# Two chunks of each SwiGLU computed with the tokens held still and turned by the DMA crossbar

## The chip, the cores and the metric

The kernel runs on one core of a Trainium2 chip. Five engines matter: TensorE (PE, matmuls; its weight loads are PEld), VectorE (DVE), ScalarE (ACT), GpSimd (POOL) and SyncE (SP), which here only starts transfers. The metric is the device time of one execution in microseconds. Before the change the median of three runs is 724.2 us (722.27 to 726.59).

## The reference, cut to what matters

One layer for 256 tokens of width 1024 in fp32: a SwiGLU, a mixer (Mamba-2 and differential attention side by side), and a second SwiGLU, each between two RMSNorms.

```
def swiglu(x, w_gate, w_up, w_down):
    return (jax.nn.silu(x @ w_gate) * (x @ w_up)) @ w_down
h = h + 0.5 * rmsnorm(swiglu(rmsnorm(h, ffn1_pre_g), ffn1_w_gate, ffn1_w_up, ffn1_w_down), ffn1_post_g)
...
h = h + 0.5 * rmsnorm(swiglu(rmsnorm(h, ffn2_pre_g), ffn2_w_gate, ffn2_w_up, ffn2_w_down), ffn2_post_g)
```

w_gate and w_up are 1024x2816, w_down is 2816x1024. The change touches only these two SwiGLUs, called f1 (0 to 187 us of the profiled execution) and f2 (537 to 722 us).

## The kernel before, in words

**Precision.** Each fp32 operand is split into a high part (an ACT cast to fp32r) and a low part (a DVE subtraction of that from the operand). A product is three matmuls: high by high, low by high, high by low. Every weight that comes in from memory therefore costs one ACT cast and one DVE subtraction per 128x1024 piece before PE can use it.

**Gate and up.** The 2816 columns are taken in eleven chunks of 256, j = 0 to 10. Chunks 0 and 1 are computed together with the tokens stationary: the normed tokens u (high and low) are the weights that PE holds, and 512 columns of w_gate or w_up stream past (`mm_nat`, L482). Their result has tokens on the partitions, but the down projection needs the columns of FF on the partitions, so it is transposed: on PE in f1, and in f2 by the DMA crossbar, which takes 16-bit elements, so that an fp32 tile goes as two planes of 16 bits (`by_dma`: planes copy L1086, transpose L1087, copy back L1091). Chunks 2 to 10 are computed with the weights stationary (`mm_runs`, `mm_part` L441): per chunk and per gate or up, 16 matmuls of 512 columns (u high and u low side by side) and 16 of 256. The result is right for the down projection at once, but it lies in two halves of a PSUM bank, which are added by an ACT copy and a DVE addition (`taken_from`, L447 and L448), two of each for gate and two for up. Then come Silu on ACT, the multiplication of up by Silu(gate) on DVE (L1127), and the split of the result into high and low (`split`, L420 cast on ACT, L421 subtraction on DVE).

**Down.** The plan for both SwiGLUs is `q1 Q2 q3 Q0 ppp`: chunks 2g and 2g+1 form quad g, and four quads are multiplied by a Strassen-Winograd scheme of seven pieces of six matmuls each (168 matmuls, L939). Chunks 8, 9 and 10 are multiplied plainly after that (L777). The pieces need sums of weight quarters. For q1 and q3 DVE makes them as they are needed (`Quad`: sums wt L128, cast wqh L136, subtraction wql L142). For Q2 and Q0 they are made early, during the chunks ("kept" sums, `stored_sums`: POOL starts the loads of ws at L221, DVE subtracts at L226, L228, L231 and L233, POOL stores to a scratch in DRAM at L229 and L234), and are reloaded later and only split (`Stored`: cast L161, subtraction L162). Which of the four steps of the kept sums is taken in which chunk stands in two tables in `ffn`, one for the middle of a chunk and one for its end.

**What sets the order.** In these stages the order on each engine comes from the tile scheduler, which follows the order of the code and of its priorities; an engine runs its own list strictly in that order. Weights are split ahead: `take()` hands out the pieces for the next matmuls and has the splits of three chunks ahead put into the lists. Tiles come from pools: k4 has 29 slots of 4 KB (all split weights, weight sums, high and low results), k2 has 7 of 2 KB, raw (incoming weights) has 3, PSUM has 3 banks pj and 5 banks bg. A tile has to wait until its slot's last reader is done. When the last chunk's multiplication has been issued, two more weight pieces are put into the lists ahead of the split of its result.

In the rows below, names end in the SwiGLU and the chunk (gh_f210 is the high result of f2, chunk 10), or in the number of the weight load and the piece (wql1173 is the low part of piece 3 of the quad whose first load is number 117; in f2 loads 115 and 116 are q1, 117 to 120 are Q2, from 121 on q3).

## Time and profile before

| what | value |
|---|---|
| median of 3 runs | 724.2 us (722.27 to 726.59) |
| profiled execution | 724.1 us, span 722.4 us, granted clock 0.999 |
| PE busy | 713.9 us (99%) |
| DVE busy | 643.3 us (89%) |
| ACT busy | 493.8 us (68%) |
| POOL busy | 60.8 us (8%) |
| f1: gate and up of chunks 8, 9, then of 10 | 98.44 to 120.67, then to 131.78 us |
| f1: the four quads | 131.78 to 169.86 us |
| f2: gate and up of chunks 8, 9, then of 10 | 626.53 to 648.76, then to 659.87 us |
| f2: the four quads | 659.87 to 699.70 us |

Rows of a timeline read: start in us, duration in us, engine, line, operation, output tile and input tile, and in square brackets the idle time before it and what ended that. Instructions of one engine overlap a little, so that the step from one start to the next (1.13 us for the 1.22 us subtractions) is what an instruction costs in a queue. A row with xN stands for N instructions that follow each other.

### The profile page before, as it was taken

Reading aid. Unit: us, or ns where it says so; the run is one execution under the profiler, and the core shown is the slowest. Engines: PE = TensorE matmul, PEld = TensorE weight load, DVE = VectorE, ACT = ScalarE, POOL = GpSimd, SP = SyncE. Lnnn points to the kernel's source line nnn. Section 1 sums busy time; section 2 is a strip of 40 time slices with the busy share of each in tenths; the row PEclk is TensorE's granted clock in tenths of the full one; section 3 lists DMA queues with packets and bytes.
Section 4 is the critical chain, followed back from the end, with each engine's and each line's share of the span. In section 5 each row is a group of like instructions: output and inputs, shape, how many; then the busy total and the mean of one; then the engine's idle time right before and its main releaser. Section 6 shows DMA issues by size and latency. Waiting matters only on the chain.

```text
span 722.4 us, 10602 instructions
## 1 busy us (share of the span) xinstructions
PE 713.9 (99%) x3925; PEld 612.7 (85%) x3925; DVE 643.3 (89%) x994; ACT 493.8 (68%) x835; POOL 60.8 (8%) x110
## 2 busy tenths in 40 slices
PE   9999999999999999999999999999999999999996
PEld 7888888888888888899888788888888889888775
DVE  6989999999979999887996998679989599898996
ACT  5666666767856777879965577795667567466572
POOL 4501110000140000000000000000021010100000
PEclk9999999999999999999999999999999999999999
DMA  8969978878574467765564664564647679975861
GB/s 295 265 213 329 319 256 287 314 265 294 175 229 129 140 212 230 233 208 177 171 220 147 206 218 137 170 193 175 235 141 256 183 234 304 331 262 224 316 221 59
DMA packets 104436, 162.06 MB, mean 224 GB/s; under 512 B 7532, under 2 KB 73664, under 8 KB 103360
## 3 DMA queue, kind: packets, MB, share of 16 engines
q1 hardware_dynamic: 92880, 135.80, 56.8%
q0 software_dynamic: 6976, 24.00, 9.5%
q10 hardware_dynamic: 4528, 1.58, 1.0%
q8 instruction: 31, 0.51, 0.3%
q14 instruction: 21, 0.17, 0.1%
HBM read 150.85 MB, written 9.47 MB: 222 GB/s over the span
## 4 chain that ended last, share of the span: by engine, by line
PE 97%; DVE 2%; issue 0%; DVEq 0%; ACT 0%; ACTq 0%
PE pup_f L441 14%; PE pg_f L441 14%; PE pxs L441 6%; PE pws L482 6%; PE pgt L482 6%; PE acc_f1p L939 5%; PE acc_f2p L939 4%; PE pn_f L498 3%; PE pbc L441 3%; PE pk L441 3%; PE pq L441 3%; PE pn_mx L482 3%; PE pwd L482 3%; PE pn_f L482 3%; PE pz L441 2%; PE acc_f1p L777 2%
## 5 line engine op out<-in xcount | busy, mean ns | idle before, releaser
L360 DVE TENSOR_TENSOR wlo<-raw,whi 128x1024 fp32r<-128x1024 f32 x204 | 244.9, 1228 | 15.6 <-ACT whi L359 14.6
L359 ACT CAST whi<-raw 128x1024 fp32r<-128x1024 f32 x204 | 206.7, 1049 | 14.0 <-DMA raw<-in_ffn_w_gate_dram 5.2
L441 PE MATMUL pup_f<-u_f,whi 128*128 128x512 f32 x288 | 68.7, 391 | 0.0
L441 PE MATMUL pg_f<-u_f,whi 128*128 128x512 f32 x288 | 68.2, 389 | 0.0
L441 PEld LDWEIGHTS pg_f<-u_f,whi 128*128 128x128 f32 x288 | 54.1, 188 | 11.2
L441 PEld LDWEIGHTS pup_f<-u_f,whi 128*128 128x128 f32 x288 | 53.0, 188 | 10.2
L441 PEld LDWEIGHTS pg_f<-u_f,wlo 128*128 128x128 f32 x288 | 36.9, 191 | 1.4
L441 PE MATMUL pup_f<-u_f,wlo 128*128 128x256 f32 x288 | 37.6, 284 | 0.0
L441 PE MATMUL pg_f<-u_f,wlo 128*128 128x256 f32 x288 | 37.4, 283 | 0.0
L441 PEld LDWEIGHTS pup_f<-u_f,wlo 128*128 128x128 f32 x288 | 35.8, 192 | 0.1
L482 PE MATMUL pgt<-whi,u_mx 128*128 128x512 f32 x128 | 33.1, 393 | 0.0
L162 DVE TENSOR_TENSOR wql<-raw,wqh 128x1024 fp32r<-128x1024 f32 x28 | 32.8, 1222 | 0.3 <-ACT wqh L161 0.3
L420 ACT CAST gh_f<-sg_f 128x512 fp32r<-128x512 f32 x18 | 11.2, 621 | 30.8 <-DVE sg_f L1127 28.9
L441 PE MATMUL pxs<-u_mx,whi 128*128 128x512 f32 x128 | 29.9, 390 | 0.0
L447 ACT COPY su_f<-pup_f 128x256 f32<-128x256 f32 x36 | 13.4, 371 | 23.0 <-PE pup_f L441 22.8
L482 PEld LDWEIGHTS pgt<-whi,u_mx 128*128 128x128 f32 x128 | 23.6, 188 | 5.3 <-issue 0.7
L136 ACT CAST wqh<-wt 128x1024 fp32r<-128x1024 f32 x16 | 16.8, 1052 | 16.1 <-DVE wt L128 14.8
L441 PEld LDWEIGHTS pxs<-u_mx,whi 128*128 128x128 f32 x128 | 23.8, 188 | 4.8
L161 ACT CAST wqh<-raw 128x1024 fp32r<-128x1024 f32 x28 | 27.4, 1048 | 0.0
L515 ACT ACTIVATE s<-s,nm 128x128 f32<-128x128 f32 (+1 forms) x32 | 14.3, 447 | 11.2 <-DVE nm L1634 9.3
L1535 DVE TENSOR_TENSOR E<-E,cbm 128x768 f32<-128x768 f32 x16 | 15.3, 957 | 6.4 <-ACT E L515 6.4
L1440 DVE SCALAR_TENSOR_TENSOR xs<-xr,cols_b,xs 128x255 f32<-128x255 f32 (+2 forms) x48 | 20.5, 480 | 0.6 <-ACT xs L1437 0.3
(500 smaller groups left out, 1703.8 us busy)
## 6 DMA issues: line engine op xcount, KB each, us to landing
raw<-in_w_in_dram SPq DMA_DIRECT2D x40, 1024.0 KB, 5.1
raw<-in_ffn_w_gate_dram SPq DMA_DIRECT2D x20, 1024.0 KB, 6.1
raw<-in_ffn_w_up_dram SPq DMA_DIRECT2D x20, 1024.0 KB, 5.7
raw<-in_ffn_w_down_dram SPq DMA_DIRECT2D x18, 1024.0 KB, 6.5
ws<-in_ffn_w_down_dram POOLq DMA_DIRECT2D x16, 512.0 KB, 6.8
sums_f<-ws POOLq DMA_DIRECT2D x16, 512.0 KB, 6.2
raw<-sums_f SPq DMA_DIRECT2D x8, 1024.0 KB, 7.0
raw<-in_ssd_w_branch_dram SPq DMA_DIRECT2D x8, 1024.0 KB, 4.9
```

The costliest lines, as they stand in the source:

```text
L136: nc.scalar.copy(hi, src)
L161: nc.scalar.copy(hi, src)
L162: nc.vector.tensor_sub(lo, src, hi.bitcast(F32))
L359: last_cast[0] = behind(nc.scalar.copy(hi, r[:, js, :]), "cast").ins
L360: m = nc.vector.tensor_sub(lo, r[:, js, :], hi.bitcast(F32))
L441: nc.tensor.matmul(to, w_(j)[:, m * P:(m + 1) * P], x_(j), start=first and j == 0, stop=not first and j == KD - 1, skip_group_check=True)
L482: nc.tensor.matmul(acc, a(k0 + j), b(j), start=first and i == 0, stop=last and i == 11)
L498: nc.tensor.matmul(accs[b], x_(k0 + j), w_(j), start=first and j == 0 and w_ is wh and x_ is acts[b][0], stop=last and j == 3 and w_ is wl)
L777: nc.tensor.matmul(acc[b][q][:, cs] if to is None else to, x_[:, ts], w_(kt)[:, halves[q]][:, cs], start=to is not None and kt == 0 and x_ ...
L939: nc.tensor.matmul(bank[p], x_, w_, start=p not in begun, stop=last and p in (1, 5, 6, 7))
L1440: nc.vector.scalar_tensor_tensor(dst[:, m, s:], acc[:, m, :T - s], cw(3 - s, c), dst[:, m, s:], ALU.mult, ALU.add)
L1535: nc.vector.tensor_tensor(E, E, cbm[g].unsqueeze(1).to_broadcast([P, 2, 3 * P]), ALU.mult)
```

## The change

Chunks 8 and 9 of both SwiGLUs are taken together with the tokens stationary, as chunks 0 and 1 are. Their four weight loads (1024 rows by 256 columns, gate and up of one chunk in turn) become four of 512 rows by 512 columns, the two of gate first, then the two of up. Gate and up each take 48 matmuls of 512 columns in two banks, one for each block of 128 tokens. Silu reads the bank directly, DVE multiplies the up bank by it, ACT copies the result into two 16-bit planes (L1163) and starts a crossbar transpose (L1164). Later (`LATER = 3` half chunks after the block's own four, at most at the end of chunk 10) the landed planes are copied back together into a tile v (two copies, L1170), and v is split by one cast (L427) and one subtraction (L428) of 128x1024. In f2 the kept sums' steps are moved one to two chunks sooner; the tables of f1 stay, but are called from the new places.

```diff
+SOONER = ("f2",)
+NATURAL, LATER = {"f1": (8,), "f2": (8,)}, 3
...
         for j in range(2, FF // T):
-            t_chunk(wg[0], 0, j * T)
-            t_chunk(wu[0], 0, j * T)
+            if j in NATURAL[tag]:
+                for w in (wg, wu):
+                    for k0 in (0, 512):
+                        s_chunk(w[0], k0, j * T)
+            elif j - 1 not in NATURAL[tag]:
+                t_chunk(wg[0], 0, j * T)
+                t_chunk(wu[0], 0, j * T)
...
+        mids = {2: (0,), 3: (0,), 4: (0, 0), 5: (1,), 6: (1, 1), 7: (2,), 8: (2, 2), 9: (3,), 10: (3, 3)}
+        ends = {2: (0,), 3: (1,), 4: (0, 1), 5: (2,), 6: (1, 2), 7: (3,), 8: (2, 3), 10: (3,)}
+        if tag in SOONER:
+            store_sums((0, 0))
+            mids = {2: (0, 1), 3: (0, 1), 4: (1, 2), 5: (2,), 6: (2, 3), 7: (3,), 8: (3,)}
+            ends = {2: (0, 1), 3: (0, 1), 4: (1, 2), 5: (2,), 6: (2, 3), 7: (3,), 8: (3,)}
...
+        def by_tokens(j):
+            sg, n = [None] * 2, 0
+            for part, bank in (("g", pj), ("u", lambda name: bg([P, 512], name))):
+                accs = [bank(f"p{part}n_{tag}{j}{b}") for b in range(2)]
+                for i in range(2):
+                    w = take()
+                    for b in range(2):
+                        bs = slice(b * P, (b + 1) * P)
+                        mm_nat(accs[b], w, (lambda k: uh(k)[:, bs], lambda k: ul(k)[:, bs]), i * 4, i == 0, i == 1, "w")
+                        if i == 1 and part == "g":
+                            sg[b] = k2([P, 512], f"sgn_{tag}{j}{b}")
+                            act(sg[b], accs[b], AF.Silu)
+                        elif i == 1:
+                            nc.vector.tensor_tensor(sg[b], accs[b], sg[b], ALU.mult)
...
+            for b in range(2):
+                planes = k2([P, 2, 512], f"np_{tag}{j}{b}", U16)
+                lands.append(k2([P, 2, 4, P], f"nl_{tag}{j}{b}", U16))
+                nc.scalar.copy(planes, sg[b].bitcast(U16).rearrange("p (c h) -> p h c", h=2))
+                nc.scalar.dma_start_transpose(lands[b].rearrange("p h m t -> p (h m) t"),
+                                              planes.rearrange("p h c -> p (h c)"))
+            gu.extend([None] * 4)
+            yield
+            v = k4([P, 4, T], f"v_{tag}{j}")
+            for b in range(2):
+                nc.scalar.copy(v[:, :, b * P:(b + 1) * P].bitcast(U16).rearrange("p m (t h) -> p h m t", h=2), lands[b])
+            gh, gl = (k4([P, 4, T], f"g{x_}_{tag}{j}", F32R) for x_ in "hl")
+            split(gh, gl, v)
...
         for j in range(2, FF // T):
+            if j in NATURAL[tag]:
+                turning[min(done_chunks[0] + 4 + LATER, 2 * (FF // T - 2))] = t = by_tokens(j)
+                next(t)
+            if j in NATURAL[tag] or j - 1 in NATURAL[tag]:
+                continue
```

The list of ACT before, in f2 at the end of chunk 10 (wqh1154 is the last high part of q1, wqh1171 and on are those of Q2):

```order
L136 CAST wqh1154_6746<-wt1154_6742 128x1024
L161 CAST wqh1171_6750<-raw117_6623 128x1024
L161 CAST wqh1172_6793<-raw118_6689 128x1024
L161 CAST wqh1173_6797<-raw118_6689 128x1024
L420 CAST gh_f210_6666<-sg_f210_6668 128x512
L161 CAST wqh1175_6824<-raw119_6814 128x1024
L161 CAST wqh1177_6828<-raw119_6814 128x1024
```

The list of ACT now, at the same place:

```order
L163 CAST wqh1171_6655<-raw117_6538 128x1024
L163 CAST wqh1172_6698<-raw118_6597 128x1024
L163 CAST wqh1173_6702<-raw118_6597 128x1024
L427 CAST gh_f210_6574<-sg_f210_6576 128x512
L1170 COPY v_f28_6708<-nl_f280_6567 128x2x4x128
L1170 COPY v_f28_6708<-nl_f281_6571 128x2x4x128
L427 CAST gh_f28_6711<-v_f28_6708 128x1024
L163 CAST wqh1175_6734<-raw119_6724 128x1024
```

The two copies that bring the turned chunks back and the cast of their high part stand between the cast of chunk 10's result and the fourth high part of Q2; f1 has the same four rows at the same place.

The list of DVE before, same place in f2 (sg_f210 is the product of up and Silu(gate) of chunk 10):

```order
L1127 TENSOR_TENSOR sg_f210_6668<-su_f210_6733,sg_f210_6668 128x512
L162 TENSOR_TENSOR wql1173_6798<-raw118_6689,wqh1173_6797 128x1024
L421 TENSOR_TENSOR gl_f210_6667<-sg_f210_6668,gh_f210_6666 128x512
L233 TENSOR_TENSOR ws011_6561<-ws011_6561 128x512
L162 TENSOR_TENSOR wql1175_6825<-raw119_6814,wqh1175_6824 128x1024
L162 TENSOR_TENSOR wql1177_6829<-raw119_6814,wqh1177_6828 128x1024
```

The list of DVE now:

```order
L1205 TENSOR_TENSOR sg_f210_6576<-su_f210_6638,sg_f210_6576 128x512
L164 TENSOR_TENSOR wql1173_6703<-raw118_6597,wqh1173_6702 128x1024
L428 TENSOR_TENSOR gl_f210_6575<-sg_f210_6576,gh_f210_6574 128x512
L428 TENSOR_TENSOR gl_f28_6712<-v_f28_6708,gh_f28_6711 128x1024
L164 TENSOR_TENSOR wql1175_6735<-raw119_6724,wqh1175_6734 128x1024
L164 TENSOR_TENSOR wql1177_6739<-raw119_6724,wqh1177_6738 128x1024
```

The low part of the turned chunks now stands ahead of all further weight subtractions, and the last step of the kept sums (ws011, L233) has left this place; it now stands some forty rows earlier, in chunk 7.

The list of ACT now, in f2 after the matmuls of chunks 8 and 9 (sgn is their product, np the planes, nl where the transpose lands; wqh115x are the high parts of q1):

```order
L138 CAST wqh1151_6577<-raw115_6462 128x1024
L1163 COPY np_f280_6566<-sgn_f280_6476 128x1024
L138 CAST wqh1152_6581<-raw116_6504 128x1024
L1164 DMA_TRANSPOSE nl_f280_6567<-np_f280_6566 128x8x128
L1163 COPY np_f281_6570<-sgn_f281_6490 128x1024
L138 CAST wqh1153_6585<-raw116_6504 128x1024
L1164 DMA_TRANSPOSE nl_f281_6571<-np_f281_6570 128x8x128
L138 CAST wqh1155_6591<-wt1155_6587 128x1024
```

And before, at that place:

```order
L136 CAST wqh1151_6669<-raw115_6516 128x1024
L447 COPY su_f29_6614<-pup_f290_6625 128x256
L447 COPY su_f29_6614<-pup_f291_6626 128x256
L136 CAST wqh1152_6673<-raw116_6572 128x1024
L136 CAST wqh1153_6677<-raw116_6572 128x1024
L420 CAST gh_f28_6452<-sg_f29_6563 128x512
L447 COPY sg_f210_6668<-pg_f2100_6691 128x256
L136 CAST wqh1155_6683<-wt1155_6679 128x1024
```

Two copies and two transposes have come in between the first four casts of q1, and three small copies and a cast of the weights-stationary form have gone or moved behind them.

More of the change, by code (lines that the diff above doesn't have):

```diff
@@ L1105, in store_sums, with first_turns @@
                     next(jobs[i])
[L1107 to L1114 removed]
+        mids = {2: (0,), 3: (0,), 4: (0, 0), 5: (1,), 6: (1, 1), 7: (2,), 8: (2, 2), 9: (3,), 10: (3, 3)}
[4 more added lines that the diff above has]
+            ends = {2: (0, 1), 3: (0, 1), 4: (1, 2), 5: (2,), 6: (2, 3), 7: (3,), 8: (3,)}
+        def first_turns(j):
             if tag in DMA_TURNS and j in (2, 3):
@@ L1123, in ffn @@
             act(sg, sg, AF.Silu)
[L1124 removed]
+            store_sums(mids.get(j, ()))
+            due()
             su = k2([P, 2, T], f"su_{tag}{j}")
@@ L1135, in ffn @@
                     even = sg
-            if first and (j == 3 or tag not in DMA_TURNS):
-                sums[0] = sums_of(0, first[0][:, :2, :], first[0][:, 2:, :])
-                del first[0]
-            store_sums({2: (0,), 3: (1,), 4: (0, 1), 5: (2,), 6: (1, 2), 7: (3,), 8: (2, 3), 10: (3,)}.get(j, ()))
+            first_sums(j)
+            store_sums(ends.get(j, ()))
+            due()
         act_table(EXP_LN)
```

41 lines of the change are left out of this document (32 added, 9 removed).

## The prediction

> **What bounds the kernel now.** I read first the busy times and the chain of work that ended last, then the waits of TensorE, and then the timelines of the engines that feed it at the two places that the change touches.
>
> ```profile
> PE 713.9 (99%) x3925; PEld 612.7 (85%) x3925; DVE 643.3 (89%) x994; ACT 493.8 (68%) x835; POOL 60.8 (8%) x110
> PE 97%; DVE 2%; issue 0%; DVEq 0%; ACT 0%; ACTq 0%
> PE acc_f2p L939 <- DVE wql L142: 1.1, 2, 0.6
> ```
>
> TensorE is on 97% of the chain, so time is won only where its own stream becomes shorter or where it stands still, and lost where something new makes it stand still. The third row is the only wait of TensorE behind the kernel's first microseconds that the view lists: in f2, the quads wait twice for low parts of weights from DVE. The stretches show how much that is (columns: the stretch's length, then busy time of PE, PEld, DVE, ACT and POOL, clock, DMA share, GB/s).
>
> ```profile
> 98.44:120.67 22.23, 22.23 (x129) 19.70 (x129) 19.76 (x28) 14.79 (x23) 2.47 (x5) 1.00 0.84 288
> 626.53:648.76 22.23, 22.23 (x130) 19.70 (x129) 19.99 (x29) 14.44 (x22) 2.84 (x6) 1.00 0.82 281
> 131.78:169.86 38.08, 38.08 (x169) 31.55 (x169) 37.72 (x38) 28.43 (x34) 0.54 (x1) 1.00 0.84 310
> 659.87:699.70 39.83, 38.71 (x169) 31.39 (x169) 39.80 (x39) 29.76 (x32) 1.07 (x2) 1.00 0.85 324
> ```
>
> The first two are chunks 8 and 9, in f1 and f2; the last two are the four quads, the same 168 matmuls each. The quads of f2 take 39.83 − 38.08 = 1.75 us longer. DVE is busy in both almost without a break (37.72 of 38.08, 39.80 of 39.83). So within the quads there are two limits a hair apart: TensorE, and DVE's list of weight subtractions. Where they meet:
>
> ```profile
> 157.91 0.39 PE L939 MATMUL acc_f1p<-wql,sh 128*128 128x512 f32 x1
> 155.99 2.48 DVE L142 TENSOR_TENSOR wql<-wt,wqh 128x1024 fp32r<-128x1024 f32 x2
> ...
> 687.58 0.50 PE L939 MATMUL acc_f2p<-wql,sh 128*128 128x512 f32 x1 [0.61 <-DVE wql L142]
> 686.29 2.49 DVE L142 TENSOR_TENSOR wql<-wt,wqh 128x1024 fp32r<-128x1024 f32 x2
> ```
>
> These are the sixth piece of q3 in f1 and in f2. In f1 the first of the two low parts is ready at 155.99 + 1.22 = 157.21 and PE needs it at 157.91: slack 0.7 us. In f2 it is ready at 687.51 and PE starts at 687.58, having stood still. After q3 the slack grows, since a piece of six matmuls costs PE 38.08 / 28 = 1.36 us and a stored piece costs DVE 1.13. So a shift D of DVE's list ahead of q3 moves f2 by D, and f1 only by what exceeds 0.7.
>
> **The change part by part.**
>
> A, the matmuls. The two chunks cost 22.23 us now, in 64 matmuls of 512 columns and 64 of 256. Afterwards there are 96 of 512. The same form runs for chunks 0 and 1:
>
> ```profile
> 536.94 8.16 PE pn_f L482 x36
> 546.20 13.65 PE pn_f L482 x60
> ```
>
> 8.16 / 36 = 0.2267 us and 13.65 / 60 = 0.2275 us each, so 96 take 21.76 to 21.84: −0.42 to −0.46 us per SwiGLU, provided that nothing waits. The weights for these chunks are split three chunks ahead in both versions (same casts and subtractions, same loads in bytes), so I add no wait there.
>
> The Trainium skill ("TensorE: Matmul & The Clock Gate", Back-to-back issue gap) gives an isolated gap of N/2.4 + 2.5 ns for a warm array; as an estimate by that page 96 × 216 ns and 64 × 216 + 64 × 109 ns would be equal, 20.8 us, and A would be nothing. The rows here (22.23 against 96 × 0.2267) do not agree, and they decide.
>
> B, what DVE and ACT no longer do. Gone per SwiGLU are eight copies L447 and eight additions L448, two multiplications L1127, two casts and two subtractions of 128x512; two Silus are replaced by two from the bank. New are two multiplications, two plane copies, two transposes, two copies back, one cast and one subtraction of 128x1024. Over the whole stage that is less work for DVE. It matters only where it stands relative to q3, so I take DVE's list in two pieces, up to chunk 10's multiplication (call its start M) and behind it.
>
> C, behind M. This is how it ran in f1 and f2:
>
> ```profile
> 138.57 0.69 DVE L1127 TENSOR_TENSOR sg_f<-su_f,sg_f 128x512 f32<-128x512 f32 x1
> 141.22 4.63 DVE L162 TENSOR_TENSOR wql<-raw,wqh 128x1024 fp32r<-128x1024 f32 x4
> ...
> 667.13 0.42 DVE L448 TENSOR_TENSOR su_f<-pup_f,su_f 128x256 f32<-128x256 f32 x1
> 667.47 1.22 DVE L162 TENSOR_TENSOR wql<-raw,wqh 128x1024 fp32r<-128x1024 f32 x1
> 668.60 0.69 DVE L1127 TENSOR_TENSOR sg_f<-su_f,sg_f 128x512 f32<-128x512 f32 x1
> 670.33 0.69 DVE L421 TENSOR_TENSOR gl_f<-sg_f,gh_f 128x512 fp32r<-128x512 f32 x1
> 670.94 0.69 DVE L233 TENSOR_TENSOR ws<-ws 128x512 f32<-128x512 f32 x1
> 671.54 4.63 DVE L162 TENSOR_TENSOR wql<-raw,wqh 128x1024 fp32r<-128x1024 f32 x4
> ...
> 669.38 0.62 ACT L420 CAST gh_f<-sg_f 128x512 fp32r<-128x512 f32 x1 [1.90 <-DVE sg_f L1127]
> 669.90 3.90 ACT L161 CAST wqh<-raw 128x1024 fp32r<-128x1024 f32 x4
> ...
> L1091 ACT COPY g_f<-gt_f x2: 1377/1379/1381, 575.0 to 577.3; 128x1024 uint16<-128x1024 uint16 x2
> ```
>
> From M to the four stored subtractions it took 141.22 − 138.57 = 2.65 us in f1 and 671.54 − 668.60 = 2.94 in f2. Now ACT, in its fixed order, does the cast of chunk 10 (starts M + 0.78, next M + 1.30), two copies back of 1.38 less 0.1 of overlap (the last row is the same copy in chunks 0 and 1) to M + 3.86, and a cast of 1.05 to M + 4.9. Then DVE subtracts 128x1024 (1.13) and comes to the stored pieces at M + 6.1: later by 3.1 us in f2, by 3.5 in f1. In the row of four behind it the weights' casts stand behind the same copies, so they are no way around. Queued behind DVE's wait are all remaining low parts of the quads, and PE waits for those. What would hide this is slack in DVE's list, and there is next to none: 0.7 us in f1, nothing in f2.
>
> The last transpose is long through by then: in ACT's list it stands ahead of a cast that ran some 13 us before M, at 655.49 in f2, and in chunks 0 and 1 the transposes landed after this long (min, median, max), as one of two whose issue holds ACT:
>
> ```profile
> L1086 ACT COPY gp_f<-sg_f2b x2: 1047/1048/1049, 564.7 to 567.1; 128x1024 uint16<-128x1024 uint16 x2
> L1087 ACTq DMA_TRANSPOSE gt_f<-gp_f x2: 1247/1248/1248, 565.8 to 568.2; - x2
> DMA to landing us min/median/max: 2.8/3.4/4.0
> ```
>
> D, up to M. In f2 the way there is this:
>
> ```profile
> 646.77 0.69 DVE L228 TENSOR_TENSOR ws<-ws,ws 128x512 f32<-128x512 f32 x1
> 652.03 1.23 DVE L142 TENSOR_TENSOR wql<-raw,wqh 128x1024 fp32r<-128x1024 f32 x1 [1.20 <-ACT wqh L136]
> 654.18 1.23 DVE L128 TENSOR_TENSOR wt<-raw 128x1024 f32<-128x1024 f32 x1 [0.93 <-DMA sums_f<-ws]
> ...
> 645.68:655.49 9.81, 9.81 (x58) 8.67 (x57) 7.43 (x11) 4.60 (x7) 0.54 (x1) 1.00 0.58 211
> 646.77:668.60 21.83, 21.83 (x113) 18.72 (x112) 19.45 (x25) 13.32 (x18) 0.54 (x1) 1.00 0.65 246
> ```
>
> From 646.77 to M DVE was idle 21.83 − 19.45 = 2.4 us. Its work there shrinks: L228 and L231 of the kept sums move to earlier chunks (0.6 us each in the queue, as 670.33 to 670.94), two L448 (0.34 each, 667.13 to 667.47), one L1127 and one L421 (0.6 each) go, 3.1 us; two multiplications of 0.6 come: −1.9. Of the idle time, 0.93 us was a weight sum waiting for a pool slot that a kept sum held until its store landed, which the sooner steps end; 1.20 was a cast behind a weight load. But ACT gets more to do between the first casts of q1: two copies of 0.95 and two transposes of 1.25, 4.4 us, for three copies and a cast of the old form (1.3 us), in a stretch where it was idle 9.81 − 4.60 = 5.2. Bounds for M in f2: −4.3 if all idle time goes, −0.6 if the transposes hold casts so that 1.3 of new idle time comes. I take −2.6, since most of the extra ACT work fits into its idle time and only the casts of the second weight load stand directly behind a transpose.
>
> In f1, DVE's way to M had no break from 119.64 on:
>
> ```profile
> 119.64 1.22 DVE L142 TENSOR_TENSOR wql<-raw,wqh 128x1024 fp32r<-128x1024 f32 x1
> 120.77 0.69 DVE L231 TENSOR_TENSOR ws<-ws,ws 128x512 f32<-128x512 f32 x1
> 121.49 0.69 DVE L233 TENSOR_TENSOR ws<-ws 128x512 f32<-128x512 f32 x1
> ```
>
> Here too L231 and L233 move ahead, and L448, L1127 and L421 go, some 3.1 us against 1.2 of multiplications. But the last kept sums are stored late in f1 (no sooner tables), and a weight sum may wait for the slot as it did in f2. Bounds −3.1 and +0.3; I take −2.2.
>
> The sum. f2: D = −2.6 + 3.1, about +0.6, and PE ends by DVE's list, so +0.6 (bounds: −4.3 + 3.1 = −1.2 and +2.5). f1: D = −2.2 + 3.5 = +1.3, less the slack 0.7: +0.6 (bounds: +0.4 − 0.7, so about −0.3, and +3.1). A's gain is swallowed in both, because PE then waits for DVE in q3. Together +1.2 us on the profiled 724.1, which lies 0.1 below the median of the runs: **725.3 us**.
>
> The Trainium skill ("VectorE: DVE Perf Modes", The three transpose paths) would turn on TensorE wherever the result may lie in PSUM, and use the crossbar otherwise. That speaks against this form, since the split could read PSUM. No run has it for these chunks yet; what it would be, by the turn of chunks 0 and 1 in f1, stands in the next row.
>
> ```profile
> 35.88 1.03 PE L1077 MATMUL pt_f<-ident,sg_f1b 128*128 128x128 f32 x8
> ```
>
> It would cost PE about 1 us per SwiGLU, more than A, but none of the copies and transposes on ACT: 724.1 + 2 × (1.0 − 0.46) = 725.2 without any DVE stall gone. The choice moves cost from one limit to the other and changes no chance here.
>
> **The rivals.**
>
> Gain. PE keeps A in both (−0.9) and DVE comes to q3 no later than before, so that part of f2's 1.75 goes. For it: idle and work before M shrink. Against: the 3.1 and 3.5 us behind M stand in fixed lists. With M at its early bounds it is −0.3 − 1.2: 722.6; with the turn's work wholly covered and no stall at all, −0.9 − 1.75: 721.4. Chance 0.17.
>
> Loss. The two copies back and the cast hold DVE's list, and M does not come earlier, because transposes on ACT hold the casts that DVE needs before M. Place: gl_f28 ahead of the fourth piece of Q2; price 3.5 − 0.7 = 2.8 in f1 and 3.1 in f2, at most 5.9: 730.0. It decides for M later than about −1 us. Halfway it is 728. For it: DVE is the second limit and has no room. Against: 3.1 us of DVE work is certainly gone. Chance 0.22.
>
> Nothing. The shifts before and behind M cancel, and PE neither gains nor waits more: 724.1. Chance 0.18; the forecast itself, +0.5 to +2.5, has 0.43.
>
> **How the numbers follow.** A measurement of this kernel tells about 0.5%, 3.6 us, from no change. No case reaches 720.6 except by a shift in the runs themselves, since A and the whole stall are 2.65 us: faster 0.07. Slower needs over 727.8, the larger half of the loss rival and some of the forecast's upper end: 0.17. Same: 0.76. The range takes in the gain with its floor and half of the loss: 721.6 to 728.2.
>
> **What would show it.** Right: in the profile after, matmuls of chunks 8 and 9 at 0.227 us, 21.8 for the pair (A); on DVE in both SwiGLUs an idle time of some 2 us before the 128x1024 subtraction L428, put down to ACT's cast L427 (C); M earlier by about 2 us relative to the start of the quads (D); waits of TensorE for low parts L144 in q3, now in f1 as well. Wrong: no such waits in f1 and a quad stage near 38.1 us in both (gain), or waits of more than 2 us in each (loss), or waits inside chunks 8 to 10, which I hold to be free of them.

## The result, and the profile after

The change made the kernel slower: 732.48 us median of six runs (730.18 to 736.01) against 725.1 (722.27 to 727.49), a ratio of 1.0119 with a 95% interval of 1.0088 to 1.015. The forecast was 725.3 us, with 721.6 to 728.2 as its range. The profiled execution took 733.6 us, with a span of 731.9.

The page of the changed kernel, engines and chain, and then the view of TensorE's waits (total, times, longest, in us):

```profile
PE 716.7 (98%) x3861; PEld 609.5 (83%) x3861; DVE 638.1 (87%) x976; ACT 497.8 (68%) x825; POOL 61.9 (8%) x110
PE 85%; DVE 5%; ACT 4%; DMA 4%; issue 2%; SPq 0%; DVEq 0%; ACTq 0%
...
PE pg_f L448 <- ACT whi L366: 3.1, 1, 3.1
PE acc_f1p L946 <- DVE wql L144: 1.6, 3, 0.6
PE acc_f1p L946 <- DVE wql L164: 0.7, 1, 0.7
PE acc_f2p L946 <- ACT wqh L138: 0.6, 1, 0.6
PE acc_f1p L784 <- DVE wlo L367: 0.5, 1, 0.5
```

Before, this view had a single row of waits behind the kernel's start; now it has these five and three more of 0.2 to 0.4 us, and the chain goes through DVE, ACT and DMA for 13% of the span. The chain's shares do not say where the time went: the lengths of the stretches do. Here are the same cuts as in the prediction, of the changed kernel (length, then busy time of PE, PEld, DVE, ACT, POOL, clock, DMA share, GB/s):

```profile
98.58:120.34 21.76, 21.76 (x98) 18.02 (x97) 17.02 (x21) 12.94 (x15) 2.92 (x6) 1.00 0.86 310
637.53:659.29 21.76, 21.76 (x98) 18.02 (x97) 16.20 (x19) 13.18 (x16) 1.02 (x2) 1.00 0.75 269
131.46:173.70 42.24, 39.55 (x169) 31.13 (x169) 39.79 (x41) 33.35 (x38) 0.54 (x1) 1.00 0.79 288
670.40:709.48 39.08, 38.48 (x170) 31.38 (x169) 36.48 (x35) 29.97 (x32) 0.54 (x1) 1.00 0.81 294
173.70:192.46 18.76, 17.91 (x83) 14.30 (x82) 17.12 (x25) 10.98 (x22) 0.00 (x0) 1.00 0.77 247
542.24:637.53 95.29, 92.01 (x492) 79.20 (x491) 80.09 (x127) 58.51 (x95) 12.84 (x23) 0.98 0.81 250
```

The first two rows are chunks 8 and 9: 21.76 us instead of 22.23 in both SwiGLUs, without a wait. Then the quads of f1 (42.24 instead of 38.08), those of f2 (39.08 instead of 39.83), the plain chunks and the end of f1, and last the way from the start of f2 to its chunk 8, in which the change alters no matmul. For those last two, the rows of the kernel before:

```profile
169.86:187.18 17.32, 17.32 (x82) 14.46 (x82) 16.99 (x25) 10.85 (x22) 0.00 (x0) 1.00 0.79 262
536.94:626.53 89.59, 89.59 (x491) 78.15 (x491) 77.20 (x123) 58.31 (x95) 8.80 (x18) 1.00 0.77 244
```

The +9.5 us of span of this execution are accounted for, within 0.1 us, by −0.47 twice for the matmuls, +4.16 in f1's quads, +1.44 in f1's end, +5.70 before chunk 8 of f2, and −0.75 in f2's quads (9.6 together). In f1, this stands behind the longer quads. First DVE, then ACT, of the changed kernel:

```profile
115.26 0.69 DVE L230 TENSOR_TENSOR ws<-ws,ws 128x512 f32<-128x512 f32 x1 [3.47 <-DMA ws<-in_ffn_w_down_dram]
124.87 1.23 DVE L130 TENSOR_TENSOR wt<-raw 128x1024 f32<-128x1024 f32 x1 [2.45 <-DMA sums_f<-ws]
139.41 0.68 DVE L1205 TENSOR_TENSOR sg_f<-su_f,sg_f 128x512 f32<-128x512 f32 x1
144.45 1.23 DVE L428 TENSOR_TENSOR gl_f<-v_f,gh_f 128x1024 fp32r<-128x1024 f32 x1 [2.35 <-ACT gh_f L427]
145.59 4.62 DVE L164 TENSOR_TENSOR wql<-raw,wqh 128x1024 fp32r<-128x1024 f32 x4
160.35 2.48 DVE L144 TENSOR_TENSOR wql<-wt,wqh 128x1024 fp32r<-128x1024 f32 x2
...
140.77 2.56 ACT L1170 COPY v_f<-nl_f 128x1024 uint16<-128x1024 uint16 x2
143.37 1.05 ACT L427 CAST gh_f<-v_f 128x1024 fp32r<-128x1024 f32 x1
```

From chunk 10's multiplication (139.41) to the stored pieces (145.59) it is 6.18 us; the forecast was 6.1. The multiplication itself is not 2.2 us earlier but 0.84 later (138.57 before). DVE stood still twice ahead of it: 3.47 us for a load that a kept sum is made from, and 2.45 us when a weight sum waited for the slot of a kept sum whose store had not landed. The pair of q3 that started at 155.99 before now starts at 160.35, 4.4 us later: that is the 0.84, and the 3.53 by which the way from the multiplication to the stored pieces has grown.

In f2 the same two rows of DVE are these:

```profile
675.19 0.69 DVE L1205 TENSOR_TENSOR sg_f<-su_f,sg_f 128x512 f32<-128x512 f32 x1
681.32 4.62 DVE L164 TENSOR_TENSOR wql<-raw,wqh 128x1024 fp32r<-128x1024 f32 x4
```

Here too it is 6.13 us from one to the other, 3.2 more than before. But the quads shrink by 0.75 us all the same, because the multiplication now starts 4.9 us behind their first matmul instead of 8.9, 3.9 sooner. How much of that is work that went away, and how much is that DVE got ahead while TensorE lost 5.70 us before chunk 8, this trace does not tell.

That loss of TensorE begins with the two transposes of chunks 0 and 1, which the change doesn't touch. They took this long (the view of the tile they land in, then ACT's and PE's timelines, all of the changed kernel):

```profile
L1094 ACTq DMA_TRANSPOSE gt_f<-gp_f x2: 1302/3156/5009, 571.1 to 573.5; - x2
DMA to landing us min/median/max: 13.4/13.8/14.3
...
585.47 1.37 ACT L1098 COPY g_f<-gt_f 128x1024 uint16<-128x1024 uint16 x1 [2.44 <-DMA gt_f<-gp_f]
602.01 1.20 PE L448 MATMUL pg_f<-u_f,whi 128*128 128x512 f32 x4 [3.07 <-ACT whi L366]
```

They landed after 13.4 to 14.3 us instead of 2.8 to 4.0, and the second held ACT 5.01 us at its issue. ACT's copies, casts and all weights behind them became late, and PE stood still for 3.07 us at the start of chunk 5. And then the clock (the same columns as above):

```profile
602.00:604.00 2.00, 1.97 (x6) 1.34 (x7) 2.00 (x3) 2.00 (x3) 0.00 (x0) 0.81 0.04 8
604.00:606.00 2.00, 2.00 (x7) 1.52 (x6) 2.00 (x3) 1.34 (x3) 0.00 (x0) 0.50 0.14 14
606.00:608.00 2.00, 2.00 (x10) 1.69 (x9) 2.00 (x4) 0.08 (x1) 0.00 (x0) 0.84 0.85 271
608.00:610.00 2.00, 2.00 (x19) 2.00 (x18) 1.55 (x3) 1.74 (x3) 0.00 (x0) 1.00 1.08 377
```

For about 3 us behind the wait, TensorE had half its clock: the 16 matmuls of 512 columns that follow take 5.7 us instead of 3.6. The page's row of busy PE shows none of that, since a slow matmul counts as busy.

### The profile page after: what moved, and what is told of

It reads as the page before. It is cut to its first block, busy times and chain, and to the rows that moved or that the text cites. A ratio compares the mean times of both kernels' runs of the same rounds, so it can differ in the third digit from the quotient of the medians.

```text
span 731.9 us, 10461 instructions
## 1 busy us (share of the span) xinstructions
PE 716.7 (98%) x3861; PEld 609.5 (83%) x3861; DVE 638.1 (87%) x976; ACT 497.8 (68%) x825; POOL 61.9 (8%) x110
## 4 chain that ended last, share of the span: by engine, by line
PE 85%; DVE 5%; ACT 4%; DMA 4%; issue 2%; SPq 0%; DVEq 0%; ACTq 0%
PE pg_f L448 9%; PE pup_f L448 8%; PE pxs L448 6%; PE pws L489 6%; PE pgt L489 6%; PE pbc L448 3%; PE pk L448 3%; PE pq L448 3%; PE pn_mx L489 3%; PE pwd L489 3%; PE pn_f L489 3%; PE pun_f L489 3%; PE pgn_f L489 3%; PE pn_f L505 3%; PE pz L448 2%
## 5 line engine op out<-in xcount | busy, mean ns | idle before, releaser
L448 PE MATMUL pg_f<-u_f,whi 128*128 128x512 f32 x224 | 55.0, 398 | 3.1 <-ACT whi L366 3.1
L448 PEld LDWEIGHTS pg_f<-u_f,whi 128*128 128x128 f32 x224 | 43.1, 193 | 12.9 <-ACT whi L366 3.9
L448 PE MATMUL pup_f<-u_f,whi 128*128 128x512 f32 x224 | 53.4, 391 | 0.0
L448 PEld LDWEIGHTS pup_f<-u_f,whi 128*128 128x128 f32 x224 | 41.2, 188 | 8.0
L448 PE MATMUL pup_f<-u_f,wlo 128*128 128x256 f32 x224 | 29.5, 284 | 0.2 <-DVE wlo L367 0.2
L448 PEld LDWEIGHTS pg_f<-u_f,wlo 128*128 128x128 f32 x224 | 28.7, 191 | 1.1
L448 PE MATMUL pg_f<-u_f,wlo 128*128 128x256 f32 x224 | 29.1, 283 | 0.0
L448 PEld LDWEIGHTS pup_f<-u_f,wlo 128*128 128x128 f32 x224 | 27.9, 192 | 0.5 <-DVE wlo L367 0.4
L427 ACT CAST gh_f<-sg_f 128x512 fp32r<-128x512 f32 x14 | 8.7, 622 | 25.3 <-DVE sg_f L1205 24.0
L454 ACT COPY su_f<-pup_f 128x256 f32<-128x256 f32 x28 | 10.4, 375 | 20.2 <-PE pup_f L448 15.6
```

The source lines that it names most:

```text
L448: nc.tensor.matmul(to, w_(j)[:, m * P:(m + 1) * P], x_(j), start=first and j == 0, stop=not first and j == KD - 1, skip_group_check=True)
L454: nc.scalar.copy(dst, acc[:, T:])
```

## The experiments

Ratios are to the kernel before, of runs on the same chip. Lengths of stretches are from one profiled execution of each, first matmul of a stretch to first matmul of the next; "end" is from the first plain matmul to the mixer (f1) or to the last matmul (f2). A profiled execution need not be near the median of its kernel: that of "only f1" was the slowest of six (730.8 us, median 727.7), and that of "f2 later" the fastest of twelve (721.7, median 723.0). So a stretch tells where one execution lost time, and the ratio what the kernel loses.

| run | ratio (95%) | f1: 8, 9 / quads / end | f2: to chunk 8 | f2: 8, 9 / quads / end |
|---|---|---|---|---|
| before | 1 | 22.23 / 38.08 / 17.33 | 89.59 | 22.23 / 39.83 / 16.27 |
| the change | 1.0119 (1.0088, 1.015) | 21.76 / 42.25 / 18.76 | 95.29 | 21.76 / 39.07 / 16.27 |
| sums not sooner | 1.0103 (1.0072, 1.0135) | 21.76 / 42.60 / 18.53 | 89.59 | 21.76 / 41.61 / 18.00 |
| only sums sooner | 1.0046 (1.0029, 1.0063) | 22.23 / 38.08 / 18.09 | 94.33 | 22.23 / 38.08 / 16.27 |
| only f1 | 1.0067 (1.0047, 1.0087) | 21.76 / 43.88 / 18.64 | 89.59 | 22.23 / 38.16 / 18.39 |
| only f2 | 1.0062 (1.0032, 1.0092) | 22.23 / 38.08 / 17.33 | 89.59 | 21.76 / 41.79 / 20.31 |
| late turn | 1.013 (1.0109, 1.0151) | 21.76 / 42.77 / 21.77 | 89.59 | 21.76 / 39.42 / 20.39 |
| late turn, packed sums | 1.0172 (1.0152, 1.0191) | 21.76 / 41.31 / 21.58 | 89.59 | 21.76 / 41.07 / 20.71 |
| packed sums | 1.0113 (1.0092, 1.0133) | 21.76 / 43.14 / 18.58 | 89.59 | 21.76 / 43.29 / 16.29 |
| only packed sums | 1.0035 (1.0014, 1.0055) | 22.23 / 38.09 / 19.68 | 89.59 | 22.23 / 38.65 / 16.37 |
| change, loads in order | 1.0113 (1.0084, 1.0142) | 21.76 / 41.67 / 18.75 | 94.52 | 21.76 / 39.29 / 16.31 |
| late turn, in order | 1.0084 (1.0051, 1.0116) | 21.76 / 38.11 / 20.07 | 89.59 | 21.76 / 39.50 / 20.41 |
| the same, packed sums | 1.0079 (1.0058, 1.0101) | 21.76 / 38.39 / 19.85 | 89.59 | 21.76 / 38.61 / 20.76 |
| the same, gain early | 1.0025 (1.0013, 1.0038) | 21.76 / 40.27 / 18.03 | 89.59 | 21.76 / 39.93 / 16.97 |
| late, in order, gain early | 1.0003 (0.9995, 1.0012) | 21.76 / 39.06 / 18.05 | 89.59 | 21.76 / 38.11 / 16.91 |
| before, gain early | 1.0004 (0.9995, 1.0014) | 22.23 / 38.08 / 17.35 | 89.59 | 22.23 / 38.65 / 16.30 |
| turn in place, rest mended | 1.0099 (1.0085, 1.0113) | 21.76 / 43.29 / 17.38 | 89.59 | 21.76 / 42.31 / 16.30 |
| f2 late | 0.9997 (0.9985, 1.0009) | 22.23 / 38.08 / 17.45 | 89.59 | 21.76 / 38.75 / 16.95 |
| f2 later | 0.9993 (0.9979, 1.0007) | 22.23 / 38.08 / 17.33 | 89.59 | 21.76 / 38.08 / 16.60 |
| both later | 1.001 (0.9998, 1.0023) | 21.76 / 39.48 / 18.37 | 89.59 | 21.76 / 38.08 / 16.88 |

### The change in its parts

Four kernels take the change apart. The sums at their old times:

```diff
-SOONER = ("f2",)
+SOONER = ()
```

> The change with the kept sums of f2 at their old times. Theory A (the sooner sums put a load and a store of DRAM beside the crossbar transposes of chunks 0 and 1 of f2, which then land after 13.4 to 14.3 us instead of 2.8 to 4.0, and PE loses about 5.7 us by chunk 5): the transposes gt land in 3 to 5 us again, no wait of PE in chunks 3 to 5; f1 unchanged at +5.3 us over before (start of the mixer at 192.5). In f2 the last kept sum is late again, so that DVE's list comes to q3 3 to 4 us later: f2 +3 to +4, in all 732 to 734. Theory B (the slow transposes come from something else, such as the five microseconds by which f2 starts later, or chance): gt lands in 13 us here as well, and with the late sums added the time is 736 to 738.

The sums alone:

```diff
-NATURAL, LATER = {"f1": (8,), "f2": (8,)}, 3
+NATURAL, LATER = {"f1": (), "f2": ()}, 3
```

> Only the kept sums of f2 sooner, all chunks with the weights stationary. Theory A: gt lands in 13 to 14 us, PE waits some 5 us for a cast in chunks 3 to 5 of f2, less the 1 to 1.75 us of stall in the quads that the later PE and the earlier sums take away: 728 to 729.5. Theory B: gt lands in 3 to 4 us, and only the quads' stall shrinks: 722.5 to 724.

One SwiGLU alone, sums at their old times:

```diff
-SOONER = ("f2",)
-NATURAL, LATER = {"f1": (8,), "f2": (8,)}, 3
+SOONER = ()
+NATURAL, LATER = {"f1": (8,), "f2": ()}, 3
```

> Chunks 8 and 9 with the tokens stationary in f1 alone, sums as before. If f1's loss is all its own (copies back and cast behind the last multiplication, 6.2 us until the stored pieces instead of 2.65; a weight sum that waits 2.45 us for the slot of a kept sum's store; later loads for the plain chunks): f1 ends 5.3 us later and the time is 729 to 730, f2 as before with its 1.75 us of stall. If part of it was of that one execution: 726 to 728.

and the same with `{"f1": (), "f2": (8,)}`:

> Chunks 8 and 9 with the tokens stationary in f2 alone, sums as before. Theory A: transposes of chunks 0 and 1 land in 3 to 4 us, no wait in chunks 3 to 5; DVE's list comes to q3 later by 3 us (copies back and cast) and by up to 1 us of the late kept sum: 727 to 729, with waits for low parts in q3 and Q0 as in f1. Theory C (in f2 the earlier multiplication of chunk 10 pays for the copies, as I had forecast): 724.5 to 725.5.

The landing of the transposes of chunks 0 and 1 decides between theories A and B. Sums not sooner, then only the sums sooner:

```profile
L1094 ACTq DMA_TRANSPOSE gt_f<-gp_f x2: 1248/1248/1249, 570.8 to 573.1; - x2
DMA to landing us min/median/max: 3.1/3.5/3.9
```

```profile
L1094 ACTq DMA_TRANSPOSE gt_f<-gp_f x2: 3139/3320/3502, 566.3 to 570.9; - x2
DMA to landing us min/median/max: 10.3/11.8/13.3
```

Theory A holds on where the transposes land and what follows. In all runs without the sums ahead of chunk 2 the stretch up to chunk 8 of f2 is 89.59 us, in the three with them 94.3 to 95.3. The times came out a little below what was expected with it: 731.2 us instead of 732 to 734 without the sooner sums, 726.9 instead of 728 to 729.5 with them alone. What lies beside the transposes shows in GpSimd's timeline of the changed kernel (started by the two rows, a store of kept sums and the load of the next ones):

```profile
572.91 0.53 POOL L236 DMA_DIRECT2D sums_f<-ws  x1 [3.86 <-DVE ws L235]
573.44 0.54 POOL L223 DMA_DIRECT2D ws<-in_ffn_w_down_dram  x1
```

Before, the first store after the transposes' issue (565.8 and 568.2) started at 577.5, when they had landed. The weight load before the transposes also started 28 us after f2's start instead of 25, so that it landed 7.6 us after the first transpose's issue instead of 3.0; which of the three transfers weighs most was not tried. The view of DMA for these microseconds counts 2112 packets for the transposes' 0.52 MB, beside the weight queue's 4247 for 4.27 MB. The Trainium skill ("DMA: Bandwidth & Descriptors", Queues, rings and completion order, the part on arbitration) says that a DMA engine takes turns between queues packet by packet. Whether the small packets are why the transposes were the ones to be late is not shown: no run varied them.

Taking the sooner sums out gains almost nothing (1.0103 against 1.0119), which looks as if they were harmless. They are not: alone they cost 0.46%. In the change, TensorE came to f2's quads late already when the copies back held DVE, so that the second loss was hidden behind the first; without the first, it shows (quads 41.61, end 18.00). Between the two SwiGLUs nothing of that kind is shown: alone they are 1.0067 and 1.0062, and 1.0129, the sum of both losses, lies inside the interval of both together. Theory C (f2 pays for its copies itself) fell with 1.0062, for sums at their old times.

### The turn later

Next, with the sums at their old times, I moved the copies back, the cast and the subtraction into q3 and Q0, one step behind each of the sixth, seventh, eighth and twelfth piece that the quads take, where ACT had been idle between its casts. The packed tables bring the last kept sums a few instructions sooner without any transfer ahead of chunk 2.

```diff
-SOONER = ("f2",)
+SOONER = ()
+LATE = {"f1": (6, 7, 8, 12), "f2": (6, 7, 8, 12)}
...
             v = k4([P, 4, T], f"v_{tag}{j}")
             for b in range(2):
+                if b and LATE.get(tag):
+                    yield
                 nc.scalar.copy(v[:, :, b * P:(b + 1) * P].bitcast(U16)...
...
+                yield
+                nc.scalar.copy(gh, v)
+                yield
+                nc.vector.tensor_sub(gl, v, gh.bitcast(F32))
...
             for p in LAST if last else FIRST:
                 wh, wl = take()
+                taken_here[0] += 1
+                if taken_here[0] in late_steps:
+                    next(late_steps.pop(taken_here[0]))
```

> Chunks 8 and 9 with the tokens stationary in both SwiGLUs, kept sums at their old times, but the two copies back, the cast and the subtraction of the turned chunks one by one inside q3 and Q0, where ACT was idle between its casts, instead of together behind chunk 10's multiplication. Theory D (the wait of DVE for those copies and that cast, 2.4 us in f1 and 2.6 in f2, with the 128x1024 subtraction, is most of the loss of 4 to 5 us per SwiGLU, and late loads for the plain chunks follow from it): the four stored pieces start some 2.6 us after the multiplication as before, no waits for low parts in q3 in f2, ratio to before 0.997 to 1.001. Theory E (the loss comes from what lies ahead of the multiplication: planes copies and transposes between the casts, the other weight loads): waits of PE in q3 and the plain chunks stay, ratio 1.005 to 1.010.

With the packed tables, where the turn is late:

```diff
+            mids = {2: (0,), 3: (0,), 4: (0, 0), 5: (1, 1), 6: (1, 2), 7: (2, 2), 8: (3, 3)}
+            ends = {2: (0,), 3: (1,), 4: (0, 1), 5: (1, 2), 6: (2, 3), 7: (2, 3), 8: (3, 3)}
```

> As the late turn, and the last kept sums a few instructions sooner in both SwiGLUs, without a transfer ahead of chunk 2. If the 2.45 us that a weight sum of f1 waited for the slot of a kept sum still count: the wait is gone and the multiplication of chunk 10 in f1 comes 1.5 to 2.5 us sooner; ratio 0.995 to 0.999, 0.001 to 0.002 below the late turn alone. If not: the same ratio as the late turn.

with them and the turn in its place:

> The turn where the change has it (behind chunk 10), the last kept sums a few instructions sooner, none ahead of chunk 2. Theory D: without the slot wait f1 loses 2.8 to 3.3 us instead of 5.3, f2 keeps its 4 us; transposes of chunks 0 and 1 land in 3 to 4 us; ratio 1.007 to 1.009 beside 1.0103 with the sums at the old times. If the slot wait were the whole of f1's loss: 1.004.

and with them alone:

> All chunks with the weights stationary, only the last kept sums a few instructions sooner and none ahead of chunk 2. The 0.93 us that a weight sum of f2 waited for a kept sum's slot goes, and a part of the 1.75 us stall in q3: ratio 0.998 to 1.000. If any sooner store collides with other transfers as the sums ahead of chunk 2 did (1.0046): above 1.002.

The late turn did not help (1.013), nor did the packed sums with it (1.0172) or in the change as it is (1.0113, where 1.007 to 1.009 was expected). The weight sum's wait for a slot in f1 was gone with them, as expected, but the multiplication stood no nearer to the quads than before the change, since DVE waited for casts of weights that had landed late instead (3.3 and 1.3 us in the change with packed sums). The packed sums alone cost 0.35% where no loss was expected; in that profile the last weights of f1 landed after 8.0 us and its end is 19.68 us, but what makes that kernel slower in general is not settled. Both theories on the turn's place looked wrong. The trace of the late turn told why. DVE and ACT of it, at the end of chunk 10 in f1:

```profile
144.49 4.81 DVE L165 TENSOR_TENSOR wql<-raw,wqh 128x1024 fp32r<-128x1024 f32 x4 [1.84 <-ACT wqh L164]
...
143.41 2.00 ACT L164 CAST wqh<-raw 128x1024 fp32r<-128x1024 f32 x2 [1.98 <-DMA raw<-sums_f]
```

The copies were gone from there, but the casts now waited for the reload of the kept sums. SyncE had started that late. SyncE of the kernel before, then of the late turn (a row with x2 holds two starts):

```profile
118.52 10.17 SPq L341 DMA_DIRECT2D raw<-in_ffn_w_down_dram  x2
130.90 1.25 SPq L341 DMA_DIRECT2D raw<-sums_f  x2
```

```profile
107.86 27.30 SPq L349 DMA_DIRECT2D raw<-in_ffn_w_down_dram  x5
135.27 0.89 SPq L349 DMA_DIRECT2D raw<-sums_f  x2
```

In every kernel so far with the new form and the old or packed sums, the scheduler puts the first load of q3 ahead of the two reloads on SyncE. That load waits for a slot, and the reloads behind it wait with it: 135.27 instead of 130.90. In the change as it is this happens in f1 only (134.70). It was hidden there because the copies back ended within a microsecond of the reload's landing. So one more dependency holds the loads to the order of the code:

```diff
+                if i - 1 in homes and i not in homes:
+                    tc.add_manual_dep(d.ins, last_load[0], order, reason="behind the kept sums")
+                last_load[0] = d.ins.name
```

In the change as it is:

> The change, with SyncE's loads held to the order of the code: in f1 the two reloads of the kept sums stand again ahead of the first load of q3 (in the change they stand behind it, start at 134.7 instead of 130.9 and land at 143 to 144). Theory F (in f1 two things end within a microsecond of each other before the fourth stored piece: the reload that has moved behind another load on SyncE, and the copies back with their cast on ACT; mending one leaves the other): the reloads start at about 131.5, the stored pieces still start some 6.2 us after the multiplication, f1 loses 4.5 to 5.3 us as before, ratio 1.009 to 1.012. Theory G (the reload alone is the cause): f1 loses 1 us or less, ratio 1.004 to 1.007.

with the late turn:

> The late turn (copies and cast spread over q3, kept sums at their old times) with the reloads of the kept sums in both SwiGLUs ahead of the next load, as before the change. Theory F: both walls are gone, the four stored pieces start 2.4 to 2.7 us after the multiplication, the list of DVE comes to q3 about 1 us late in f1 and 1 to 2 us early in f2, ratio 0.997 to 1.003, against 1.013 with the late turn alone. Theory E (what lies ahead of the multiplication costs most): ratio above 1.007.

and with the packed sums as well:

> As the late turn in order, with the last kept sums a few instructions sooner. Theory F: the weight sum's wait for a slot in f1 (2.45 us in the change) shrinks to under 0.5, the multiplication comes 1.5 to 2 us sooner, no waits for low parts in q3; ratio 0.995 to 1.000. If the loads of the plain chunks (5 to 8 us from issue to landing, 1.3 us of wait with the sums sooner and no other change) decide: 1.002 to 1.006.

In order alone: no gain (1.0113), as theory F had it. In order and late: f1's quads take 38.11 us, against 42.25 in the change, 42.77 with the late turn alone and 41.67 in order alone. So in f1 each of the two walls by itself hid the other. In f2 the late turn alone had already brought the quads from 41.61 to 39.42, and in these profiles the order adds nothing to that (39.50). The ratio falls to 1.0084, far from the 0.997 to 1.003 that theory F gave and over the 1.007 from which theory E was to hold; its interval also overlaps those of the kernels beside it. The table shows where the rest sits, and it is not ahead of the multiplication: the ends, 20.07 and 20.41 us instead of 17.33 and 16.27. With the packed sums as well it is 1.0079, which neither of the two expectations had.

### The load of the gain

ACT and GpSimd of the late turn in order, in the plain chunks of f1:

```profile
172.11 1.99 ACT L373 CAST whi<-raw 128x1024 fp32r<-128x1024 f32 x2 [4.19 <-DMA raw<-in_ffn_w_down_dram]
163.69 0.53 POOL L764 DMA_DIRECT2D pg_f<-in_ffn_post_g_dram  x1 [46.27 <-PE acc_f1p L957]
```

The cast that waited for the last weight load, started at 164.37, could begin only 7.7 us later. A 512 KB load, the norm's gain to all partitions, had been started 0.7 us ahead of it, when its slot came free. In the four profiled kernels with the late turn and the gain there, both SwiGLUs, the last weights took 7.4 to 7.9 us; in the profiled execution of before, where they started 0.1 to 0.2 us ahead of the gain, 5.2 and 5.3. The lead of 0.7 us is not all of it: with the gain 0.02 to 0.04 us behind them they took 5.7 to 8.1 in five other places (f2 of "sums not sooner", "only f1" and "only f2", both SwiGLUs of "only packed sums"). The clock of the same kernel in f2 behind that wait:

```profile
709.00:711.00 2.00, 2.00 (x7) 1.53 (x6) 1.90 (x4) 0.00 (x0) 0.00 (x0) 0.56 0.00 0
711.00:713.00 2.00, 2.00 (x7) 1.58 (x6) 1.78 (x4) 0.21 (x1) 0.00 (x0) 0.59 0.00 0
713.00:717.00 4.00, 4.00 (x19) 3.28 (x18) 1.91 (x4) 1.54 (x6) 0.00 (x0) 1.00 0.00 0
```

So the load of the gain was moved ahead of the quads, in four kernels:

```diff
+        pg = load_gain(post_v, f"pg_{tag}")
         acc, rest, combine, pairs, begin = mm_quads(gu, sums, tag)
-        pg = load_gain(post_v, f"pg_{tag}")
```

> The late turn in order with the last kept sums a few instructions sooner, and the load of the norm's gain (512 KB to the 128 partitions, started by GpSimd) ahead of the quads instead of beside the last weight load of the plain chunks. Theory H (with both waits in front of the quads gone, what is left is that load: where it starts 0.7 us before the last weight load, the weights land 7.4 to 7.9 us after their issue instead of 4.7 to 5.4, PE waits 1.2 to 1.7 us for a cast and then runs at half clock for some 3 us, 4 to 5 us in both SwiGLUs together): the last weight loads land in 4.7 to 5.5 us, no wait of PE over 1 us in the plain chunks, ratio 0.995 to 1.001. Theory I (those landing times are chance or come from another transfer): waits and half clock stay, ratio 1.006 to 1.010.

> As the run above with the kept sums at their old times. Theory H: ratio 0.996 to 1.002 (against 1.0084 with the gain beside the last weight load), the stall of f2 in q3 still under 0.8 us. Theory I: 1.006 to 1.010.

> The kernel before, with only the gain's load moved ahead of the quads. Theory H: before lost nothing to it in its profiled run (the weights landed 1.3 us before PE needed them) but may in others: ratio 0.997 to 1.000. If a slot that the gain holds during the quads costs weights their lead: 1.001 to 1.005.

> The turn where the change has it, behind chunk 10's multiplication, with everything else mended: reloads of the kept sums ahead of the next load, no sums ahead of chunk 2, the last kept sums a few instructions sooner, the gain's load ahead of the quads. This prices the copies back and their cast by themselves. Theory F: DVE waits 2.3 to 2.6 us for the cast in each SwiGLU, the stored pieces start 6.2 us after the multiplication, PE loses 2 to 3 us in the quads of each: ratio 0.005 to 0.008 above the run with the late turn, 1.003 to 1.007. If the turn's place does not matter once the rest is mended: the same ratio as the late turn within 0.002.

Theory H holds: with the gain early the last weights land in 4.6 to 4.9 us, the ends are 16.3 to 18.1 us, no run of them has half a clock there, and the late turn in order is level with before (1.0003). The packed sums cost 0.2% beside it (1.0025, outside the 0.995 to 1.001 expected); why is not settled. Before itself gains nothing from the earlier gain (1.0004). And the fourth prices the turn's place with all else mended: 1.0099. DVE of that kernel, at the end of chunk 10 in f1 and in f2:

```profile
139.88 0.69 DVE L1234 TENSOR_TENSOR sg_f<-su_f,sg_f 128x512 f32<-128x512 f32 x1
144.86 1.23 DVE L435 TENSOR_TENSOR gl_f<-v_f,gh_f 128x1024 fp32r<-128x1024 f32 x1 [2.29 <-ACT gh_f L434]
146.00 4.62 DVE L165 TENSOR_TENSOR wql<-raw,wqh 128x1024 fp32r<-128x1024 f32 x4
...
671.84 0.68 DVE L1234 TENSOR_TENSOR sg_f<-su_f,sg_f 128x512 f32<-128x512 f32 x1
676.80 1.23 DVE L435 TENSOR_TENSOR gl_f<-v_f,gh_f 128x1024 fp32r<-128x1024 f32 x1 [2.54 <-ACT gh_f L434]
677.94 2.35 DVE L165 TENSOR_TENSOR wql<-raw,wqh 128x1024 fp32r<-128x1024 f32 x2
```

6.1 us each from the multiplication to the stored pieces. With the late turn and otherwise the same (1.0025) that is 1.0099 − 1.0025 = 0.7%, about 5.3 us for the place of four instructions: the upper part of the 0.5 to 0.8% expected. The ratio itself lies above the expected 1.003 to 1.007, since the kernel with the late turn beside it has 1.0025 already.

### Whether the gain can be had

The last three ask for a kernel that beats both, with the loads in order and the gain early: the late turn in f2 alone, the same with the subtraction behind the first plain weights, and that in both SwiGLUs.

```diff
-NATURAL, LATER = {"f1": (8,), "f2": (8,)}, 3
-LATE = {"f1": (6, 7, 8, 12), "f2": (6, 7, 8, 12)}
+NATURAL, LATER = {"f1": (), "f2": (8,)}, 3
+LATE = {"f2": (6, 7, 8, 12)}
```

> Chunks 8 and 9 with the tokens stationary in f2 alone, late turn, reloads in order, gain's load early, sums at their old times. The trace of the run with both SwiGLUs late and the gain early has f2 at 21.76 us for the two chunks, 38.1 for the quads and 16.9 for the rest, against 22.23, 39.8 and 16.3 before, and f1 at 21.76, 39.1, 18.05 against 22.23, 38.1, 17.3. So f2 alone should gain 0.47 + 1.7 - 0.6, about 1.5 us: ratio 0.997 to 0.999 if the gain is real and repeats; 1.000 if it is within what landing times of the loads scatter.

```diff
-LATE = {"f2": (6, 7, 8, 12)}
+LATE = {"f2": (6, 7, 8, 19)}
```

> As f2 alone, with the 128x1024 subtraction moved behind the first weights of the plain chunks, so that it no longer stands ahead of the stored pieces of Q0 whose end frees the slot of the last weight loads: the rest behind the quads 16.3 to 16.5 us instead of 16.9, ratio 0.996 to 0.998, or the same as the run above.

```diff
-NATURAL, LATER = {"f1": (), "f2": (8,)}, 3
-LATE = {"f2": (6, 7, 8, 19)}
+NATURAL, LATER = {"f1": (8,), "f2": (8,)}, 3
+LATE = {"f1": (6, 7, 8, 19), "f2": (6, 7, 8, 19)}
```

> As that, in both SwiGLUs: f1 at 21.76, 38.1 to 39.1 and 17.3, ratio 0.995 to 0.998 if the two half gains (0.9 us on PE, up to 1.7 of the stall in f2) can be had, 0.999 to 1.001 if the last waits of f1 stay.

0.9997, 0.9993 and 1.001: none is clear of before. In f2 the profile of the second has what was hoped for, 21.76, 38.08 and 16.60 us, 1.9 us less than the profiled execution of before. That would be 0.26%, a ratio of 0.9974. The measured interval, 0.9979 to 1.0007, holds no change and ends just short of that. The stall in f2's quads is itself not the same in every execution: 39.83 us before, but 38.16 in "only f1" and 38.65 in "before, gain early", where f2's chunks and quads are the old ones. In f1 a loss of 1 to 2 us in quads and end stays; its cause was not tried.

## Why the prediction was wrong

Three steps failed: the gain of D in f1, the slack behind q3, and the moved kept sums, whose transfers stood at nothing in the sum. The sign came out as forecast (slower), but not by its terms: instead of +0.6 in each SwiGLU, the profiled execution has about +5.1 in f1 and +4.5 in f2.

**A, the matmuls: right.** 21.76 us, as forecast, wherever a SwiGLU has the new form, with no wait in chunks 8 to 10.

**C, behind the multiplication: right in size, 6.18 us in f1 and 6.13 in f2 against 6.1 forecast,** and the run with all else mended shows that its place costs about 0.7% in both SwiGLUs together.

**D, up to the multiplication: wrong in f1.** I let the instructions that went away pull the multiplication 2.6 us (f2) and 2.2 us (f1) ahead. In f1 it came 0.84 us later, and 1.15 later relative to the quads' first matmul, outside the bounds I had set (−3.1 to +0.3). The 2.2 was also more than its own terms give: 3.1 gone less 1.2 added is 1.9, and the list had no idle time to lose. It looked unbroken before, but it was full rather than bounding: what stood at its head was a load, the casts behind it and a pool slot held by a kept sum. With 1.9 us of work gone, DVE waited 3.47 us for the load and 2.45 us for that slot instead. I had named the slot and then counted all of the saved work. It was not this one execution, and not the slot alone: in all thirteen profiles with the new form in f1 the multiplication starts 7.1 to 9.8 us behind the quads' first matmul, against 7.0 before, in the five with packed sums too, where the wait for the slot is gone.

With the measured D the sum of this part comes out: 1.15 + 3.53 − 0.7 = 4.0 us for f1's quads (4.16 measured), and −3.94 + 3.19 = −0.75 for f2's (−0.75 measured). But in f2 DVE could also get ahead while TensorE lost its 5.70 us, so no run tells whether −2.6 would have been right without it. In "only f2", which keeps the sums at their old times, it is −1.3; but in "only f1", where nothing in f2 is changed, it is −1.6, so an execution can move it by as much as that.

**"After q3 the slack grows": wrong.** I followed DVE's list to q3 and stopped. The stored pieces behind it end the use of the slots that the last weight loads wait for, and those take 5 to 8 us to land. PE waited there in most of the kernels with the new form; f1's end cost 1.44 us in the change itself. It takes the gain's load beside them, which I did not consider at all: with the turn in its place and the gain early, the last weights of f1 start no sooner (38.3 us behind the quads' first matmul, 37.2 in the change), and the end is 17.38 us against 17.33 before. The order and the packed sums by themselves did not do that (18.75 and 18.58).

**The moved kept sums: I counted their DVE work and the slot that they free, and not the transfers that they start.** That is +5.70 us in f2, the largest single loss, with no rival of mine near it: a store, a load and a later weight load beside two transposes, 13.8 us instead of 3.4, then a wait of 3.07 us, then half a clock.

**SyncE's order** was another miss: in f1 the reloads had moved behind a load, and I did not price it. It did not decide the change's own time, as the run with the loads in order shows (1.0113), but it hid what the copies cost until it was mended.

**The rivals.** The loss that I gave 0.22 (730.0) was the nearest. Its mechanism is what the runs show in f1, at more than its price: 42.24 − 38.08 = 4.2 in the quads against 2.8, because D's gain was missing and some 1 us was added. In f2 it lay under the other loss. The gain (0.17) needed an earlier multiplication that did not come. And "at most 5.9" was no upper end: it held only what one mechanism could do.

**The Trainium skill's rule** to turn on TensorE where PSUM will do ("VectorE: DVE Perf Modes", Rules for kernel authors) was not tried for these chunks, so it stays open whether that form would have come out level.

## What to carry to other kernels

When an instruction leaves a list that is full, ask what the next one waits for besides its turn: a load, a pool slot or another queue's order takes the place, and the saved time turns into a wait. Moving a step moves the transfers that it starts, so list what will be in flight beside them at the new place, above all transposes and the load that the bounding engine needs next. Where two waits end within a microsecond of each other, mending either one alone shows nothing, and a run with everything but the suspect mended prices it.
